# TensorE's order written by hand in three more places of a two-block layer

## The chip, the cores and the metric

The kernel runs on one core of a Trainium2 chip. Time is the device time of one execution in microseconds (us); of several runs the median counts, and the profiled execution is one further run. The engines are TensorE (PE: matmuls; PEld: its weight loads), VectorE (DVE), ScalarE (ACT), GpSimd (POOL) and the DMA queue that SyncE (SP) issues to. Each engine takes its instructions in the order in which the program has them. An instruction that waits holds up everything behind it on its engine.

## The reference, cut to what matters

512 tokens of width 1024 go through two blocks, in float32:

```python
h = h + 0.5 * swiglu(rmsnorm(h, ffn1_norm), ...)          # FFN1
h = h + (gated fox, dsa and memory attention) @ w_out     # Mix1; km, vm = split(rmsnorm(mem) @ w_mem_kv)
h = h + 0.5 * swiglu(rmsnorm(h, ffn2_norm), ...)          # FFN2

p = rms_norm(x, pre_mix_norm) @ w_in                      # Mix2: q, k, v, z of GDN; z, x, B, C, dt of SSD
q, k, v = silu(causal_dwconv(q, k, v))                    # four taps
g = -exp(gdn_a_log) * softplus(a + gdn_dt_bias)
o_a = rms_norm(gdn_chunked(l2n(q), l2n(k), v, g, beta)) * silu(z_a)
o_s = rms_norm((ssd_chunked(x, dt, B, C) + d * x) * silu(z_s))   # dt = softplus(...)
x = x + rms_norm(concat(o_a, o_s) @ w_out, post_mix_norm)
u = causal_dwconv(rms_norm(x, pre_ffn_norm) @ w_up)       # last feed-forward, ffn_conv, three taps
out = x + rms_norm((silu(gate) * up) @ w_down)
```

## The kernel before

Activations lie with the features on the 128 partitions and the 512 tokens along the free axis. Every float32 product is made of three matmuls on operands that are split into a high and a low part: `mm3` issues whi x xh, whi x xl and wlo x xh (L163, L168, L169). One such step, 128 x 128 weights on 512 tokens, is the unit in which this text counts: "a step" is three matmuls.

`wload` fetches 512 KB of weights by an SP DMA into `raw` (two buffers), ScalarE casts them to `whi` (L157) and VectorE subtracts to get `wlo` (L158). Where `k.lo` is set to `nc.gpsimd`, GpSimd makes the `wlo` instead. A block of eight steps (24 matmuls) uses one such load. SP issues its DMAs in program order too: a load that waits for a free `raw` buffer holds back every DMA behind it.

The stages, with their times in the profiled execution: FFN1 (to about 600 us), Mix1 (600 to 942), FFN2 (to 1308), Mix2 (to 1847), and `ffn_conv` (to the end). In FFN1 and FFN2, `ffn` runs 11 pairs of columns; the first pair goes through `gemm_wide`, and the norm's scale `R` is spread over the partitions by four small matmuls, `pb`. Between FFN1's pairs a generator `then` advances by one piece: setup and the loads of `mem`; `rest()`, which turns 75 rows of gains (fetched by 19 small DMAs, tile `rows`, L80 to L83) with one transpose, L88; then `mem_kv`, which transposes and splits the memory tokens (`pm`, `mm`, `my`), and makes memory keys and values.

Mix2's `gates` makes the small projections `psm`, the norm (`pn`, `ry` on GpSimd, `pb`), the softplus on VectorE (L250 to L261), `g`, its cumulative sums `pc` (four matmuls, L1400) and the table of rows `prow`. `gdn_k` and `gdn_a` make the keys and the 8 decay tables `A`, from which `blocks32` inverts small triangles on GpSimd by way of DRAM; `inverses` goes on from there on TensorE (`p1` at L1586). Then come the scans, the SSD part, the norms, the gates by `z` (whose product with `q` or `xs` is on GpSimd), the split of the result into `oa` and `os`, and `w_out`. `ffn_conv` opens with another norm.

What sets the order: everywhere but in Mix1 the framework's scheduler orders each engine's instructions by priorities that follow the order of the code; Mix1 has its TensorE order written out, under `manual_schedule`, with small pieces between product steps. Under `manual_schedule(engines={PE})` TensorE follows the code literally.

Of the kernel before, what the change touches and what calls it, by code (L numbers as in the profile page):

```python
# [4 lines left out]

# [6 lines left out]
F32R = mybir.dt.float32r  # L12
# [15 lines left out]
class K:  # L28
# [150 lines left out]
    def gemm_steps(self, w, c0, ncols, x, evac, kmax=4, after=None):  # L179

        nk = len(x)
# [81 lines left out]
    def sumsq(self, xs):  # L263

        nc = self.nc
        acc = None
        for x in xs:
            sq = self.tmp("sq")
            nc.scalar.activation(sq, x, AF.Square)
            if acc is None:  # L270
                acc = sq
            else:
                nc.vector.tensor_add(acc, acc, sq)
        return [acc]
# [53 lines left out]
    def ffn(self, h, gain, wg, wu, wd, norms=None, then=iter(())):  # L328
# [18 lines left out]
        for f0 in range(0, nff, 2):  # L347
# [16 lines left out]
            if f0 == 0:  # L364
                self.gemm_wide([(wg, 0), (wu, 0)], y, (ev_gate, ev_up), rows())
            else:
                self.gemm_fm(wg, f0 * 128, 256, y, ev_gate)
                self.gemm_fm(wu, f0 * 128, 256, y, ev_up)
            next(then, None)
# [147 lines left out]
class Mix1:  # L517
# [428 lines left out]
    def turned_evac(self, out, R):  # L946
# [4 lines left out]
        def ev(m, ps):  # L951
            t = k.tmp("vf")[:, :nb * 128]
            nc.vector.tensor_mul(t, ps[:, :nb * 128], R)
            pt = k.ps("tv")
            for b in range(nb):
                nc.tensor.transpose(pt[:, b * 128:(b + 1) * 128], t[:, b * 128:(b + 1) * 128], k.ident)
            nc.scalar.copy(out[:, :, m * 128:(m + 1) * 128], pt[:, :nb * 128].rearrange("p (b c) -> p b c", b=nb))
# [13 lines left out]
    def mem_kv(self, xt):  # L971
# [4 lines left out]
        for c in range(DC):  # L976
# [9 lines left out]
            y.append((hi, lo))  # L986
        r = k.norm_of(k.token_sumsq(xt), D)
        yield
        Rm = k.spread(r)
        kmt = k.kt.tile([128, 4, ml], F32, name="km")  # L990
# [8 lines left out]
        self.head_norm(km, self.head_stats(km, 4, 128, 128), 128, k.c("mqg"))  # L999
        self.km = km  # L1000
        vmt = k.kt.tile([128, 2, 512], F32, name="vm")
        yield from self.gemm_half(w, 512, 512, y, self.turned_evac(vmt, Rm))
# [272 lines left out]
class Mix2:  # L1275
# [25 lines left out]

    def ztile(self):
# [41 lines left out]
    def row(self, i=None, pick=None):  # L1344


        ps = self.k.ps("row", "r")
# [21 lines left out]
    def gates(self):  # L1369
# [7 lines left out]
        self.rt = k.norm_of(k.row_sums(k.sumsq(self.h)), D)  # L1377
        self.R = k.spread(self.rt)
        f = k.tmp("smf")
        nc.scalar.copy(f[:32], ps[:32])  # L1380
        pt = k.ps("smt")
# [14 lines left out]
        k.load_consts("cums")  # L1396
        pc = k.ps("pc")
# [29 lines left out]
        pt = k.ps("prow")  # L1427
# [5 lines left out]
        nc.vector.tensor_copy(self.pick, k.c("pick"))  # L1433

# [4 lines left out]
    def gdn_k(self, hf):  # L1439
        k, nc, a = self.k, self.nc, self.a  # L1440
        self.st[hf] = {"k": []}
# [7 lines left out]
        k.gemm_fm(a["w_in_2"][0], 1024 + hf * 512, 512, self.y, ev_k)  # L1449

    def gdn_qv(self, hf):
        k, nc, a = self.k, self.nc, self.a
        win = a["w_in_2"][0]
        st = self.st[hf]
        st["q"], st["v"] = qt, vb = self.big("q"), self.big("vb")

        def ev_q(m, ps):
            self.gconv(hf * 4 + m, ps, qt[:, m])

        def ev_v(m, ps):  # L1460
            t = k.tmp("vf", tag="f")
            self.gconv(16 + hf * 4 + m, ps, t)
            pt = self.turned(t, "a")
            for b in range(NB):
                nc.scalar.activation(vb[:, m, b * 128:(b + 1) * 128], pt[:, b * 128:(b + 1) * 128], AF.Copy,
                                     scale=self.vscale[:, b, hf * 4 + m:hf * 4 + m + 1])

        k.gemm_fm(win, hf * 512, 512, self.y, ev_q)
        k.gemm_fm(win, 2048 + hf * 512, 512, self.y, ev_v)

    def gdn_a(self, hf):
        k, nc = self.k, self.nc
        st = self.st[hf]
        ks = st["k"]

        (x, xv), (r, rv), (t, tv), (_, b2) = (self.per_head("kn" + c) for c in "xrtb")
        st["kd"] = []
        for m in range(4):

            pt, kd = self.turned(ks[m], "b"), k.tmp("kd", tag="kd")  # L1480
            self.sums_turned(xv[:, :, m:m + 1], pt)
            for b in range(NB):
                s = slice(b * 128, (b + 1) * 128)
                nc.scalar.activation(kd[:, s], pt[:, s], AF.Copy, scale=self.dec[:, b, hf * 4 + m:hf * 4 + m + 1])
            st["kd"].append(kd)
# [8 lines left out]
        for m in range(4):  # L1494
            hh = hf * 4 + m
# [3 lines left out]
            nc.scalar.activation(d1, d1, AF.Exp, scale=-1.0)  # L1499
            pkk = k.ps("pkk", "b")  # L1500
            for b in range(NB):
# [3 lines left out]
                                               op0=ALU.mult, op1=ALU.mult)  # L1505

    def gdn_qe(self, hf):

        k, nc = self.k, self.nc
        st = self.st[hf]  # L1510
        qt = st["q"]
        st["qe"] = qe = self.per_head("qe")[0]
        x, xv = self.per_head("qx")
        for m in range(4):
            self.sums_turned(xv[:, :, m:m + 1], self.turned(qt[:, m], "b"))
        nc.vector.tensor_scalar(qe, x, EPS, 128.0 * EPS, op0=ALU.add, op1=ALU.mult)

    def gdn_qk(self, hf):
        k, nc = self.k, self.nc
        st = self.st[hf]  # L1520
# [502 lines left out]
```

## Time and profile before

| | us |
|---|---|
| runs | 2233.55, 2235.99, 2236.47 |
| median | 2235.99 |
| profiled execution | 2238.18, of which its span 2236.5 |
| TensorE busy | 2173.7 (97% of the span) |
| VectorE busy | 1255.2 (56%) |
| ScalarE busy | 933.8 (42%) |
| GpSimd busy | 325.1 (15%) |
| mean granted clock of TensorE | 0.991 |

The busy time is the sum of an engine's instructions; what is missing to the span is time in which it waits. The granted clock is 1.00 at 2.4 GHz and 0.50 at 1.2 GHz. Views used here are the list of waits (who waited for whom, summed), the timeline (instructions in order of time, with the idle time before each and what ended it), and the windows (busy time of each engine in a given stretch).

### The profile page before, as it was taken

The page shows a single profiled execution, that of the slowest core. Times are in us where ns is not written, and L with a number is a line of the kernel's source. Part 1 is how long each engine was busy: PE and PEld are TensorE (multiplying, and loading weights), DVE is VectorE, ACT ScalarE, POOL GpSimd, SP SyncE. Part 2 cuts the span into 40 slices and gives each one's busy share as a digit, 9 for nine tenths or more (in the row PEclk, how much of TensorE's full clock was granted, in tenths as well). Part 3 has the DMA queues.
Part 4 walks back from the last instruction along what each step waited for, and adds up shares of the span by engine and source line. Part 5 has one row for each costly group of instructions (what it writes and reads, how often), then busy time and mean ns, then how long its engine had stood idle before and what let it go on. Part 6 is the DMA issues. An engine that isn't in the chain of part 4 may idle for free. (4 is left out here: it accounts for less than half of the span.)

```text
span 2236.5 us, 27895 instructions
## 1 busy us (share of the span) xinstructions
PE 2173.7 (97%) x10700; PEld 1759.4 (79%) x10700; DVE 1255.2 (56%) x2155; ACT 933.8 (42%) x1537; POOL 325.1 (15%) x340
## 2 busy tenths in 40 slices
PE   8999999999999999999999999999999898999998
PEld 6788888777677777788888877878777787888887
DVE  4544433575699654544343347866677526777623
ACT  4333322355555444332322237554556525444421
POOL 0110100011122222011110021550312100000000
PEclk9999999999999999999999999999999998999999
DMA  4233333322222223333333332331122223333332
GB/s 152 86 113 104 95 109 113 94 67 69 69 85 72 66 76 95 113 89 102 95 95 108 113 88 76 86 111 39 56 67 57 76 94 113 95 96 103 95 94 94
DMA packets 198508, 202.39 MB, mean 90 GB/s; under 512 B 19556, under 2 KB 184063, under 8 KB 198375
## 3 DMA queue, kind: packets, MB, share of 16 engines
q1 hardware_dynamic: 197607, 198.12, 29.8%
q0 software_dynamic: 768, 2.49, 0.4%
q8 instruction: 84, 1.38, 0.3%
q14 instruction: 49, 0.40, 0.1%
HBM read 192.70 MB, written 7.88 MB: 90 GB/s over the span
## 5 line engine op out<-in xcount | busy, mean ns | idle before, releaser
L163 PE MATMUL pg<-yh,whi 128*128 128x512 f32 x1856 | 745.6, 402 | 5.9 <-ACT yh L225 2.3
L169 PE MATMUL pg<-yh,wlo 128*128 128x512 f32 x1856 | 730.2, 394 | 1.2 <-DVE wlo L158 1.1
L168 PE MATMUL pg<-yl,whi 128*128 128x512 f32 x1856 | 729.7, 393 | 0.0
L158 DVE TENSOR_TENSOR wlo<-raw,whi 128x1024 fp32r<-128x1024 f32 x341 | 423.7, 1243 | 517.7 <-ACT whi L157 513.7
L157 ACT CAST whi<-raw 128x1024 fp32r<-128x1024 f32 x349 | 362.1, 1038 | 633.2 <-PE pg L168 429.7
L163 PEld LDWEIGHTS pg<-yh,whi 128*128 128x128 f32 x1856 | 350.3, 189 | 81.7 <-issue 9.1
L169 PEld LDWEIGHTS pg<-yh,wlo 128*128 128x128 f32 x1856 | 349.9, 189 | 75.4 <-DVE wlo L158 2.9
L168 PEld LDWEIGHTS pg<-yl,whi 128*128 128x128 f32 x1856 | 350.3, 189 | 67.5 <-issue 2.5
L163 PE MATMUL pg<-hidh,whi 128*128 128x512 f32 x352 | 138.7, 394 | 0.0
L169 PE MATMUL pg<-hidh,wlo 128*128 128x512 f32 x352 | 138.0, 392 | 0.0
L168 PE MATMUL pg<-hidl,whi 128*128 128x512 f32 x352 | 136.6, 388 | 0.0
L361 POOL TENSOR_TENSOR hp<-ut,sg 128x512 f32<-128x512 f32 x44 | 73.3, 1667 | 424.1 <-DVE ut L359 399.5
L217 ACT CAST hidh<-hp 128x512 fp32r<-128x512 f32 x44 | 27.3, 620 | 142.5 <-POOL hp L361 142.3
L169 PEld LDWEIGHTS pg<-hidh,wlo 128*128 128x128 f32 x352 | 66.1, 188 | 15.5
L1910 DVE SCALAR_TENSOR_TENSOR fo<-ft,fcw,fo 128x511 f32<-128x511 f32 x88 | 65.8, 749 | 21.7 <-ACT fo L1907 20.5
L168 PEld LDWEIGHTS pg<-hidl,whi 128*128 128x128 f32 x352 | 66.1, 188 | 14.8
L163 PEld LDWEIGHTS pg<-hidh,whi 128*128 128x128 f32 x352 | 66.2, 188 | 13.1
L218 DVE TENSOR_TENSOR hidl<-hp,hidh 128x512 fp32r<-128x512 f32 x44 | 30.4, 691 | 79.6 <-ACT hidh L217 79.6
L715 POOL TENSOR_SCALAR s<-s,den 128x256 f32<-128x256 f32 (+3 forms) x80 | 42.5, 533 | 190.6 <-DVE den L714 180.0
L1951 PE MATMUL pd<-whi,hidh 128*128 128x512 f32 x176 | 69.4, 394 | 0.0
L1952 PE MATMUL pd<-whi,hidl 128*128 128x512 f32 x176 | 69.4, 394 | 0.0
L1953 PE MATMUL pd<-wlo,hidh 128*128 128x512 f32 x176 | 69.2, 396 | 0.0
(502 smaller groups left out, 3000.1 us busy)
## 6 DMA issues: line engine op xcount, KB each, us to landing
raw<-in_w_in SPq DMA_DIRECT2D x100, 512.0 KB
raw<-in_ffn_w_gate SPq DMA_DIRECT2D x40, 512.0 KB
raw<-in_ffn_w_up SPq DMA_DIRECT2D x40, 512.0 KB
raw<-in_ffn_w_down SPq DMA_DIRECT2D x40, 512.0 KB
raw<-in_w_up SPq DMA_DIRECT2D x40, 512.0 KB
raw<-in_w_out SPq DMA_DIRECT2D x24, 512.0 KB
raw<-in_w_down SPq DMA_DIRECT2D x22, 512.0 KB
raw<-in_w_branch SPq DMA_DIRECT2D x12, 512.0 KB
```

The source lines that it names most:

```text
L157: nc.scalar.copy(hi, raw)
L158: (self.lo or nc.vector).tensor_sub(lo, raw, hi.bitcast(F32))
L163: first = mm(out, whi, xhi, start=start, stop=False)
L168: mm(out, whi, xlo, start=False, stop=False)
L169: mm(out, wlo, xhi, start=False, stop=stop)
L218: nc.vector.tensor_sub(lo, x, hi.bitcast(F32))
L361: nc.gpsimd.tensor_mul(p, ut, sg[m])
L715: nc.gpsimd.tensor_scalar(p[:, :w], p[:, :w], den, 1.0, op0=ALU.mult, op1=ALU.mult)
L1910: nc.vector.scalar_tensor_tensor(o[:, s:], t[:, :T - s], k.fcw[:, j:j + 1], o[:, s:], op0=ALU.mult, op1=ALU.add)
L1951: nc.tensor.matmul(pss[b], xh[:, s], hi[:, i], start=st, stop=False)
L1952: nc.tensor.matmul(pss[b], xl[:, s], hi[:, i], start=False, stop=False)
L1953: nc.tensor.matmul(pss[b], xh[:, s], lo[:, i], start=False, stop=sp)
```

## The change

FFN1's pairs from the second on are under `manual_schedule`, and `then` advances after each block of 24 matmuls instead of after each pair. The transposes of the memory values are put off by a block. Mix2's whole TensorE order is by hand: a generator `products` yields after each of 544 steps, `fill(n)` runs n of them, and small pieces stand between, directly or by `later(n, ...)`, which calls a piece n steps on. A scan makes the next state (`sc4`) before its output (`sc3`). `gdn_z(0)` and `ssd_gemms(0)` have their `wlo` on GpSimd as well: 20 such loads instead of 8. `oa` and `os` have exchanged the buffers that they are split into. At the end of Mix2, 7 matmuls of 512 columns whose result is not used (`idle`) stand ahead of `pb`, and 8 behind it. In `ffn_conv` the opening is under `manual_schedule`, its sum of squares is added up on GpSimd (7 adds), and the transposes `ph` stand between steps. TensorE's matmuls grow from 9909 to 9924, which are these 15; all others are the same ones in another order. ScalarE loads its function tables 44 times instead of 38.

```diff
 def ffn(..., then=iter(()), woven=False):
...
+        self.gemm_wide([(wg, 0), (wu, 0)], y, pair(0), rows())
+        next(then, None)
+        with self.tc.manual_schedule(engines={mybir.EngineType.PE}) if woven else ExitStack():
+            for f0 in range(2, nff, 2):
+                for w, ev in zip((wg, wu), pair(f0)):
+                    self.gemm_fm(w, f0 * 128, 256, y, ev, then=then if woven else iter(()))
...
 def turned_evac(self, out, R, turns):
...
+            def turn():
...
+            turns.append(turn)
...
 class Mix2:
+    def later(self, n, do):
+        at = self.done + n
+        i = sum(d[0] <= at for d in self.due)
+        self.due.insert(i, (at, do))
...
 def gates(self):
...
+        k.load_consts("cums")
+        yield
+        self.rt = k.norm_of(k.row_sums(acc), D)
+        yield
+        self.R = k.spread(self.rt)
...
         nc.vector.tensor_mul(g, self.dt, k.nega.unsqueeze(1).to_broadcast([128, NB, 24]))
-        k.load_consts("cums")
-        pc = k.ps("pc")
+        yield
+        pc = k.ps("pc", "b")
...
+    def idle(self, n, a, b):
+        k = self.k
+        ps = k.ps("idle", "r")
+        for _ in range(n):
+            self.nc.tensor.matmul(ps, a[0][:, :128], b[0], start=True, stop=True)
...
+        self.later(n, decay)
+        self.later(n + 2, table)
...
 def run(self):
...
+        def products():
+            k.lo = nc.gpsimd
+            yield from self.gdn_k(0)
+            yield from self.gdn_k(1)
+            k.lo = None
+            yield from self.gdn_q(0)
+            yield from self.gdn_v(0)
+            yield from self.gdn_q(1)
+            yield from self.gdn_v(1)
+            k.lo = nc.gpsimd
+            yield from self.gdn_z(0)
+            yield from self.ssd_gemms(0)
+            k.lo = None
+            yield from self.ssd_gemms(1)
+            yield from self.gdn_z(1)
+            yield from self.ssd_z()
+            yield from k.gemm_steps(a["w_out_2"][0], 0, D, self.out, ev, nk=16)
...
+            gates = self.gates()
+            next(gates)
+            for n in (3, 6, 13, 24):
+                upto(n)
+                next(gates)
+            upto(184)
+            both = [self.inverses(hf) for hf in range(2)]
+            for _ in range(7):
+                for steps in both:
+                    next(steps, None)
+                    fill(1)
+            woven(self.gdn_scan(0))
...
+            upto(298)
+            group = self.ssd()
...
+            sums = k.row_sums(sq)
+            idle(7)
+            pb = k.spread(k.norm_of(sums, D), copy=False)
+            idle(8)
...
 def ffn_conv(k, h, y, out):
+        acc = k.sumsq(h, nc.gpsimd)
+        fill(3)
+        sums = k.row_sums(acc)
+        fill(1)
+        next(turns)
+        fill(1)
+        next(turns)
+        fill(1)
+        R = k.spread(k.norm_of(sums, D))
```

TensorE in FFN1, around the transpose of the 75 gain rows. Before, it stands after 120 matmuls behind `pb`:

```order
L163 MATMUL pg_485<-yh_195,whi_518 128x512
L168 MATMUL pg_485<-yl_196,whi_518 128x512
L169 MATMUL pg_485<-yh_195,wlo_519 128x512
L88 MATMUL rows_562<-ct_base,rows_383 128x75
L979 MATMUL pm_719<-ct_base,mt_406 128x128
L979 MATMUL pm_719<-ct_base,mt_410 128x128
L163 MATMUL pg_571<-yh_167,whi_575 128x512
```

After, it stands behind 48 matmuls, the last of them those of the second pair's first load (`whi_420`); the memory's transposes follow 24 matmuls later:

```order
L164 MATMUL pg_417<-yh_179,whi_420 128x512
L169 MATMUL pg_417<-yl_180,whi_420 128x512
L170 MATMUL pg_417<-yh_179,wlo_421 128x512
L89 MATMUL rows_448<-ct_base,rows_383 128x75
L164 MATMUL pg_416<-yh_183,whi_459 128x512
L169 MATMUL pg_416<-yl_184,whi_459 128x512
L170 MATMUL pg_416<-yh_183,wlo_460 128x512
```

The transpose has moved 72 matmuls towards the start. Its DMAs stand where they stood, on SP behind the fourth load of the second pair.

VectorE in Mix2's gates, from the softplus's reciprocal (`spc`) to `g`, on which `pc` waits. Before, one `cx` (the first key's product times `R`) stands between:

```order
L253 RECIPROCAL spc_10662<-spc_10662 128x96
L254 TENSOR_TENSOR spc_10662<-spc_10662,spb_10661 128x96
L255 TENSOR_TENSOR spd_10663<-spc_10662 128x96
L256 TENSOR_SCALAR spe_10664<-spd_10663 128x96
L258 SCALAR_TENSOR_TENSOR spe_10664<-spe_10664,spd_10663 128x96 x6
L259 SCALAR_TENSOR_TENSOR spe_10664<-spe_10664,spc_10662 128x96
L261 SCALAR_TENSOR_TENSOR dt<-spe_10664,spa_10660 128x96
L1293 TENSOR_TENSOR cx_10777<-pg_10726,R_10641 128x512
L1394 TENSOR_TENSOR g_10681<-dt,nega 128x96
```

After, from the same reciprocal:

```order
L254 RECIPROCAL spc_10699<-spc_10699 128x96
L1317 TENSOR_TENSOR cx_10745<-pg_10640,R_10680 128x512
L255 TENSOR_TENSOR spc_10699<-spc_10699,spb_10698 128x96
L256 TENSOR_TENSOR spd_10700<-spc_10699 128x96
L257 TENSOR_SCALAR spe_10701<-spd_10700 128x96
L259 SCALAR_TENSOR_TENSOR spe_10701<-spe_10701,spd_10700 128x96
L1320 SCALAR_TENSOR_TENSOR kf_10744<-cx_10745,gcw,kf_10744 128x511
L259 SCALAR_TENSOR_TENSOR spe_10701<-spe_10701,spd_10700 128x96
L1320 SCALAR_TENSOR_TENSOR kf_10744<-cx_10745,gcw,kf_10744 128x510
L259 SCALAR_TENSOR_TENSOR spe_10701<-spe_10701,spd_10700 128x96
L1320 SCALAR_TENSOR_TENSOR kf_10744<-cx_10745,gcw,kf_10744 128x509
L259 SCALAR_TENSOR_TENSOR spe_10701<-spe_10701,spd_10700 128x96 x3
```

Two more rows of the softplus and then `g` follow. The `cx` has moved ahead of most of the softplus, and three of the key's convolution taps (`kf`) now stand inside it.

TensorE at `pc`. Before:

```order
L163 MATMUL pg_10804<-yh_10529,whi_10808 128x512
L168 MATMUL pg_10804<-yl_10530,whi_10808 128x512
L169 MATMUL pg_10804<-yh_10529,wlo_10809 128x512
L163 MATMUL pg_10804<-yh_10533,whi_10808 128x512
L1400 MATMUL pc_10685<-g_10681,ct_10683 128x96 x4
```

After, where `pg_10640` is the product that `cx` reads:

```order
L164 MATMUL pg_10640<-yh_10560,whi_10728 128x512
L169 MATMUL pg_10640<-yl_10561,whi_10728 128x512
L170 MATMUL pg_10640<-yh_10560,wlo_10729 128x512
L164 MATMUL pg_10641<-yh_10548,whi_10728 128x512
L169 MATMUL pg_10641<-yl_10549,whi_10728 128x512
L170 MATMUL pg_10641<-yh_10548,wlo_10729 128x512
L1435 MATMUL pc_10755<-g_10718,ct_10634 128x96 x4
```

Between `pn` and `pc` there are 30 product matmuls now and were 52, and the product that `cx` reads ends three matmuls ahead of `pc`, where it ended 16 ahead.

TensorE at the end of Mix2. Before, the last products of `w_out`, the norm's sums, the spread of its scale, and the first product of `ffn_conv`:

```order
L168 MATMUL pg_14996<-osl_14565,whi_15089 128x512
L169 MATMUL pg_14996<-slots_14543,wlo_15090 128x512
L288 MATMUL pn_15126<-ones,sq_14710 128x1 x4
L321 MATMUL pb_15142<-ct_base,ry_15139 128x128 x4
L163 MATMUL pg_15222<-yh_15153,whi_15229 128x512
```

After:

```order
L170 MATMUL pg_15001<-osh_14645,wlo_15095 128x512
L289 MATMUL pn_15131<-ones,sq_14715 128x1 x4
L1476 MATMUL idle_15143<-osh_14553,slots_14305 128x512 x7
L322 MATMUL pb_15155<-ct_base,ry_15152 128x128 x4
L1476 MATMUL idle_15160<-osh_14553,slots_14305 128x512 x8
L164 MATMUL pg_15247<-yh_15176,whi_15254 128x512
```

(`pn` has a second row of four in both.) The two groups `idle` stand where TensorE had nothing.

## Rows read from the trace of the kernel before

**Rows 1.** Windows, four stretches: elapsed, busy time by engine (x instructions), granted clock, DMA.
```profile
600.00:942.50 342.50, 337.89 (x1770) 265.65 (x1771) 234.02 (x580) 172.25 (x336) 79.82 (x113) 1.00 0.28 83
942.50:1307.80 365.30, 363.71 (x1604) 299.19 (x1603) 139.79 (x164) 104.54 (x129) 39.16 (x23) 1.00 0.33 98
1307.80:1847.00 539.20, 518.25 (x2974) 417.08 (x2973) 357.03 (x618) 286.09 (x529) 139.45 (x137) 0.99 0.26 75
1331.00:1405.80 74.80, 70.40 (x355) 56.92 (x356) 58.92 (x143) 54.83 (x145) 11.68 (x5) 1.00 0.25 71
```
**Rows 2.** List of waits, PE, 34.3 to 205.9 (total us, times, longest).
```profile
PE pg L169 <- DVE wlo L158: 1.1, 3, 0.5
PE hs L605 <- ACT hq L602: 1.1, 1, 1.1
PE pm L979 <- DVE mm L981: 1.0, 2, 0.5
```
**Rows 3.** List of waits, PE, 1307.8 to 1847.
```profile
PE pg L168 <- DVE oal L218: 4.7, 1, 4.7
PE tr L1341 <- POOL q L1670: 3.2, 5, 1.5
PE tr L1341 <- ACT vf L1298: 2.6, 2, 2.4
...
PE tr L1341 <- ACT kf L1298: 1.9, 1, 1.9
PE pc L1400 <- DMA ct<-in_consts: 1.6, 1, 1.6
```
**Rows 4.** List of waits, PE, 1847 to 1898.6.
```profile
PE pb L321 <- POOL ry L244: 3.5, 2, 1.7
```
**Rows 5.** Windows at half clock (columns as in rows 1).
```profile
171.40:174.80 3.40, 3.40 (x18) 3.40 (x17) 2.87 (x11) 0.46 (x1) 0.00 (x0) 0.50 0.04 7
...
1765.40:1772.20 6.80, 4.07 (x10) 3.20 (x11) 3.90 (x6) 1.36 (x2) 0.00 (x0) 0.50 0.00 0
1850.80:1861.00 10.20, 6.35 (x16) 4.84 (x17) 7.80 (x15) 4.74 (x8) 1.01 (x1) 0.50 0.79 272
```
**Rows 6.** Timeline, PE: start, duration, instruction, idle before it and what ended it.
```profile
2.86 0.24 PE L88 MATMUL rows<-ct_base,rows 8*128 8x8 f32 x1 [2.86 <-DMA rows<-in_ffn_norm]
...
31.84 0.60 PE L321 MATMUL pb<-ct_base,ry 128*128 128x128 f32 x4
...
206.10 0.44 PE L956 MATMUL tv<-ct_base,vf 128*128 128x128 f32 x2 [1.44 <-DVE vf L953]
```
**Rows 7.** Timeline, SP's queue (issues) in FFN1 and behind the last table.
```profile
1.25 0.35 SPq L83 DMA_DIRECT2D rows<-in_ffn_norm  x1
...
47.59 0.25 SPq L81 DMA_DIRECT2D rows<-in_dsa_k_norm  x1
...
1405.86 0.35 SPq L1552 DMA_DIRECT2D ascr<-A  x1
```
**Rows 8.** Timeline, DVE in Mix2's gates.
```profile
1322.66 0.26 DVE L254 TENSOR_TENSOR spc<-spc,spb 128x96 f32<-128x96 f32 x1
...
1323.49 3.80 DVE L258 SCALAR_TENSOR_TENSOR spe<-spe,spd 128x96 f32<-128x96 f32 x6
...
1333.67 0.73 DVE L1296 SCALAR_TENSOR_TENSOR kf<-cx,gcw,kf 128x511 f32<-128x511 f32 x1
```
**Rows 9.** Groups of instructions, DVE, 1307.8 to 1847: total busy, mean ns of one.
```profile
L158 DVE TENSOR_TENSOR wlo<-raw,whi 128x1024 fp32r<-128x1024 f32 x61 | 77.9, 1277 | 74.1 <-ACT whi L157 73.2 <-PE pg L169 0.5
...
L1504 DVE SCALAR_TENSOR_TENSOR A<-pkk,knb,d 128x128 f32<-128x128 f32 x32 | 9.7, 345 | 1.4 <-PE pkk L1503 0.9
L1359 DVE TENSOR_TENSOR d<-row,pk 128x256 f32<-128x256 f32 x24 | 9.4, 417 | 0.8 <-PE row L1350 0.8
```
**Rows 10.** Timeline, POOL in Mix2: one weight split, and the last loads of `blocks32`.
```profile
1324.18 2.40 POOL L158 TENSOR_TENSOR wlo<-raw,whi 128x1024 fp32r<-128x1024 f32 x1 [4.95 <-ACT whi L157]
...
1483.90 1.56 POOL L1572 DMA_DIRECT2D X<-xscr  x2
```

More of the change, by code (lines that the diff above doesn't have):

```diff
@@ L326, in spread, with ffn @@
         return r
-    def ffn(self, h, gain, wg, wu, wd, norms=None, then=iter(())):
+    def ffn(self, h, gain, wg, wu, wd, norms=None, then=iter(()), woven=False):
         nc = self.nc
@@ L346, in ffn, with pair @@
         hid = [None] * nff
-        for f0 in range(0, nff, 2):
+        def pair(f0):
             sg = {}
@@ L953, in ev @@
             nc.vector.tensor_mul(t, ps[:, :nb * 128], R)
[L954 to L957, printed above, removed]
+            def turn():
+                pt = k.ps("tv")
+                for b in range(nb):
+                    nc.tensor.transpose(pt[:, b * 128:(b + 1) * 128], t[:, b * 128:(b + 1) * 128], k.ident)
+                nc.scalar.copy(out[:, :, m * 128:(m + 1) * 128], pt[:, :nb * 128].rearrange("p (b c) -> p b c", b=nb))
+            turns.append(turn)
         return ev
@@ L1707, in ssd, with group @@
         free = self.slots()
-        for g in range(2):
+        def group(g):
             bm, cm = self.bc[g], self.bc[2 + g]
@@ L1764, in ssd_z @@
+        return group
     def ssd_z(self):
@@ new lines, in run, with fill, upto, woven @@
+        work = products()
+        def fill(n):
+            for _ in range(n):
+                next(work, None)
+                self.done += 1
+                while self.due and self.due[0][0] <= self.done:
+                    self.due.pop(0)[1]()
+        def upto(n):
+            fill(n - self.done)
+        def woven(steps):
+            for n in steps:
+                fill(n)
+        with self.tc.manual_schedule(engines={mybir.EngineType.PE}):
+            gates = self.gates()
[10 more added lines that the diff above has]
+            woven(self.gdn_scan(0))
+            for m in range(4):
+                self.gdn_qk(1, m, 5 * m)
+            fill(19)
+            woven(self.gdn_scan(1))
+            for hf in range(2):
+                self.gdn_norm(hf)
+                for m in range(4):
+                    self.later(16 + 10 * hf + 2 * m, partial(self.gdn_out, hf, m))
+            upto(298)
+            group = self.ssd()
+            for g in range(2):
+                woven(group(g))
+            free, tags = self.slots(F32R), iter(("A", "QK", "A", "kd") * 4)
+            def slot(s):
+                tag = next(tags)
+                return next(free) if tag == "A" else k.tmp(s, F32R, tag)
+            self.out += [k.split(self.st[hf]["q"][:, m], "oa", slot) for hf in range(2) for m in range(4)]
+            upto(416)
+            self.out += [k.split(x, "os", k.yslot) for x in self.xs[:4]]
+            upto(544)
+            idle = lambda n: self.idle(n, self.out[0], self.out[8])
+            sums = k.row_sums(sq)
+            idle(7)
+            pb = k.spread(k.norm_of(sums, D), copy=False)
+            idle(8)
@@ L1911, in conv, with pair @@
         return o
-    for f0 in range(0, nff, 2):
+    def pair(f0):
         sg = {}
@@ L1927, in ev_up, with products, fill @@
             hid[f0 + m] = k.split(o, "hid", (lambda s: k.hslot(s, F32R)) if f0 + m < 4 else None)
-        if f0 == 0:
-            k.gemm_wide([(w, 0), (w, DFF)], y, (ev_gate, ev_up), rows())
-            residual()
-        else:
-            k.gemm_fm(w, f0 * 128, 256, y, ev_gate)
-            k.gemm_fm(w, DFF + f0 * 128, 256, y, ev_up)
+        return ev_gate, ev_up
+    def products(f0):
+        for c0, ev in zip((0, DFF), pair(f0)):
+            yield from k.gemm_steps(w, c0 + f0 * 128, 256, y, ev)
+    with k.tc.manual_schedule(engines={mybir.EngineType.PE}):
+        work, turns, pss = products(2), residual(), []
+        k.gemm_wide([(w, 0), (w, DFF)], y, (lambda m, ps: pss.append(ps),) * 2)
+        def fill(n):
+            for _ in range(n):
+                next(work, None)
+        acc = k.sumsq(h, nc.gpsimd)
[7 more added lines that the diff above has]
+        R = k.spread(k.norm_of(sums, D))
+        for ev, two in zip(pair(0), (pss[:2], pss[2:])):
+            for m, ps in enumerate(two):
+                ev(m, ps)
+                fill(1)
+                next(turns, None)
+        fill(1000)
+        for _ in turns:
+            pass
+    for f0 in range(4, nff, 2):
+        for _ in products(f0):
+            pass
     wd = a["w_down_2"][0]
```

332 lines of the change are left out of this document (175 added, 157 removed).

## The prediction, made before the changed kernel was run

> **What bounds the kernel now.** I read the page's busy shares first: TensorE works 97% of the span, so what can be won is its waiting, its half-clock stretches and the switching between products and small work; all product steps stay. The windows by stage come next [rows 1]. FFN2, which the change leaves alone, shows the price of pure products: 365.3 us for 1604 matmuls, or 0.228 us each, 1.6 us idle. Mix1, whose order is by hand, idles 4.6 us of 342.5 (1.35%); Mix2 idles 539.2 - 518.25 = 20.95 us (3.9%). Then the lists of waits, which say who ends that idle time [rows 2 to 4]: an operand that VectorE, ScalarE or GpSimd hands over late, each time with ready products standing behind it in the order. Last the windows at half clock [rows 5]: after such waits TensorE is granted 0.50, that is 1.2 GHz, for 3.4 us or a multiple. The row from 171.4 stands for four of 3.4 us (the others begin at 1478.7, 1594.8 and 1884.9). TensorE busy for t us at half clock loses t/2: 1.7 us for each of the four, 2.0 for the one from 1765.4 (4.07 busy), 3.2 for the one from 1850.8 (6.35 busy).
>
> **FFN1.** What goes: the waits for wlo 1.1, hq 1.1 and mm 1.0 [rows 2], tv's 1.44 [rows 6], and the half clock from 171.4, 1.7: together 6.3. I take all of it, since 24 products (5.5 us) now lie between a memory piece and its reader. What comes: a wait at the transpose of the gain rows. TensorE leaves `pb` at about 32 [rows 6] and has 48 matmuls of 0.228, 10.9 us, before it: it arrives at 43. The last of the 19 small loads is issued at 47.59 and takes 0.25 [rows 7]; SP's order up to there is the old one, and these loads stand behind the second pair's fourth weight load, whose buffer depends on VectorE and not on TensorE's later order. From issue to use, a load of the same kind took 2.86 - 1.25 = 1.6 us [rows 6, 7]. So the rows arrive near 49.3 and TensorE waits about 6 us (4.8 if they landed at once). Before, this cost nothing, because 72 more matmuls (16.4 us) stood ahead. Clock behind it: the 4.7 us wait for `oal` [rows 3] was followed by the 2.0 us of half-clock loss [rows 5]; I take 2. Sum: 6 + 2 - 6.3 = +2 (from -5, if the loads are early after all, to +5, if the memory's denser weight loads make TensorE wait too).
>
> **Mix2, what goes.** The five large waits, oal 4.7, q 3.2, vf 2.6, kf 1.9, ct 1.6 [rows 3], are 14.0 of the 20.95. Of the other 7 I let 4 go; one that stays is the first, for FFN2's last output. The oal wait goes because the late half of the result is now last in `w_out`'s contraction; the ct wait because its load is issued earlier; the others because steps stand in between. Half clock: 1.7 + 1.7 + 2.0 = 5.4. Together -23.4.
>
> **Mix2, what comes.** First `pc`: the key's product ends three matmuls (0.7 us) ahead of it, and then VectorE has one `cx` and three taps at about 0.73, and twelve small operations from the reciprocal to `g` at about 0.28 (one is 0.26, with a little between them) [rows 8]: 2.9 + 3.4 = 6.3 us. TensorE waits some 6 us with all products behind it on the same in-order engine (3.4 us if the taps come out behind `g`, 8 if a GpSimd split falls into it, below); clock, 2. Second, `blocks32`: its chain runs from the first issue behind the last table at 1405.86 [rows 7] to the end of the last issue at 1485.5 [rows 10] and the landing, some 82 us, and TensorE's order puts 95 steps (65 us) and about 12 us of small matmuls between the last table and `p1`: a wait of 3 (0 to 6), plus 1.7 for the clock. Third, VectorE, where it has as much to do as TensorE: the tables of the k part and the SSD's first group. I set 5 (0 to 14), from the next paragraph. Sum +17.7. Net Mix2: -6 (-20 to +8). The inverses, which now alternate between the halves with a step between, and the scans I cost at nothing: products cover them, and without that cover each of their 14 pieces would show a copy of well under 1 us.
>
> **GpSimd beside VectorE.** Six softplus operations took 3.80 us where one takes 0.26 [rows 8]: while GpSimd made a weight split from 1324.18 to 1326.58 [rows 10], one of them was held for 2.2 us. Twelve more splits go to GpSimd: each takes 1.28 us off VectorE [rows 9] and may hold an operation for up to 2.2, so 12 x 0.9 = 11 us more VectorE time at worst, 15 less at best. That is where the 0 to 14 above comes from, with a further 3 us for the SSD group's denser tables; 5 is the middle of what a path that is VectorE's in parts would show.
> The Trainium skill (GPSIMD Engine Reference, Specifications) says that GpSimd shares its SBUF interfaces with VectorE and contends with VectorE instructions that have two SBUF inputs, and that speaks against this part of the change. By that rule, the trace agrees: the held operation reads two tensors. Were every split to hold VectorE on TensorE's path, the sum would be 6 us worse; were none to, 5 better.
>
> **End of Mix2 and the opening.** What goes: the second of the two waits for `pb` (half of 3.5 [rows 4]), now behind 9 products and two transposes; the half clock from 1884.9, 1.7, and from 1850.8, 3.2, if the 15 idle matmuls keep the clock up. They shorten no chain: 7 x 0.228 = 1.6 us fits into the first `pb` wait of 1.7. If the clock has already fallen when they run, they take twice that, and the two groups delay the path by 1.3 and about 1.2. What comes: the seven adds on GpSimd, which contend with VectorE while it makes `ffn_conv`'s operands: 1.5 (0 to 5). Net -5 (-6.6 to +1.5).
>
> **Sum.** +2 - 6 - 5 = -9 against the profiled execution's 2238.2, or 2229. That execution lies 2.2 us above the median of the runs, 2236.0; I forecast a median of 2227.
>
> **Rivals.**
> (a) The hand order works as in Mix1. For: it is the same method, and Mix1 idles 1.35%. Mix2 would then idle 7.3 instead of 20.95, -13.7, with its half clock gone, -5.4; FFN1 -6.3; the opening -6.6. Sum -32: 2204. Against: Mix1 had no step like `pc`, three matmuls behind its operand. Chance 0.18.
> (b) Slower: the decay tables are VectorE's. Eight tables come at every third step, that is 9 matmuls, 2.05 us, and two small ones, 2.6 in all. For one table VectorE makes two `d` (0.83), a clamp and four `A` (1.4) [rows 9], about 2.6, and beside it convolution and weight work. Before, TensorE pulled products forward; in a fixed order it cannot, and the PSUM bank of `pkk` is the stop. If VectorE is 1.5 us behind at each of the eight tables, that is 12, with clock losses of 2 and a contended `pc` (+2): 2227 + 16 = 2243. It decides as soon as VectorE needs over 1 us per table beside the table. Against: in the k part before, VectorE was busy 58.9 of 74.8 us [rows 1], which leaves room. Chance 0.18.
> (c) The idle matmuls do nothing or harm: the clock falls anyway. The opening gives -1 instead of -5, a little less than the second `pb` wait. 2231. Chance 0.15.
> (d) New waits pay back all that the old ones cost, 2236 (the two new waits of 6 us at their upper ends and `blocks32` at 6). Chance 0.13.
>
> **How the numbers follow.** My forecast, 2227, gets 0.36. The range reaches to (a) and over (b): 2206 to 2246. A measurement of this kernel tells about 0.2%, 4.5 us, from no change. Faster by more than that, below 2231.5: the forecast nearly whole (0.34), (a) 0.18, half of (c) 0.08, and a little of (d), 0.61. Within it: the rest of (c), most of (d), a part of (b), 0.20. Slower: 0.19.
>
> **What would show it.** In the profile after: a TensorE wait of about 6 us at `rows` (L89) near 43 us, ended by a DMA, and one of about 6 at `pc` (L1435), ended by VectorE's `g`, each with a half clock behind; no wait for `oal`, `vf` or POOL `q` over 1 us; a full clock through the end of Mix2, with the yh wait filled. I am wrong if `rows` doesn't wait (the loads were then issued earlier than the order suggests), if the table stretch in the k part shows TensorE waiting for `A` eight times (b), or if Mix2 is shorter by 15 us or more (a).

## The result, and the profile after

The changed kernel takes 2297.8 us (median of four runs, 2296.5 to 2300.7); the kernel before takes 2235.7 in the same series. The ratio is 1.028, with a 95% interval of 1.0265 to 1.029: slower by 62 us, where the prediction had 9 us faster.

The stages, read off the timelines, each from its first matmul to that of the next (us; FFN1 counts from the start of the span, and the last column runs from the final `pn` of the second mixer to the last matmul):

| | FFN1 | Mix1 and FFN2 | Mix2 | opening and end |
|---|---|---|---|---|
| before | 415.8 | 893.3 | 541.3 | 379.0 |
| after | 419.2 | 894.8 | 599.0 | 375.3 |

The first matmul of Mix1 is at 415.8 us in the kernel before; the 600 us that were given for it above are wrong, so the window from 600 to 942.5 in [rows 1] is only the later part of Mix1. The whole of it, from 415.8, idles 13.8 us of 526.7 (2.6%).

Nearly everything came in the second mixer. The windows of the kernel after (elapsed, busy time by engine, granted clock, DMA share, GB/s): the first feed-forward's first part, the second mixer, and in it the stretch of the decay tables.

```profile
34.30:205.90 171.60, 163.45 (x814) 137.91 (x813) 78.70 (x116) 56.94 (x83) 18.97 (x13) 0.96 0.35 105
1312.80:1909.80 597.00, 535.92 (x2974) 434.11 (x2973) 354.17 (x606) 294.95 (x535) 165.84 (x149) 0.95 0.24 68
1362.50:1448.90 86.40, 64.27 (x238) 49.72 (x237) 45.88 (x113) 46.46 (x112) 4.78 (x2) 0.80 0.13 38
```

The second line answers to the third of [rows 1]. The same 2974 matmuls took 597.0 us instead of 539.2, 57.8 more. TensorE was idle for 597.0 - 535.9 = 61.1 us, before 20.95: 40.1 more. And the matmuls themselves took 535.9 - 518.25 = 17.7 more, since the granted clock is 0.95 on the mean; in the stretch of the tables it is 0.80. VectorE's busy time has hardly changed (354 against 357), though 12 weight splits, some 15 us, have left it: other operations of its own took longer. One that takes 0.74 us elsewhere took 2.18 while GpSimd made a split:

```profile
1380.24 2.37 POOL L159 TENSOR_TENSOR wlo<-raw,whi 128x1024 fp32r<-128x1024 f32 x1 [11.07 <-ACT whi L158]
1380.98 2.18 DVE L1320 SCALAR_TENSOR_TENSOR kf<-cx,gcw,kf 128x511 f32<-128x511 f32 x1
```

What TensorE waited for in the second mixer (us in total, times, longest), to be held against [rows 3]; `tr` are the transposes of keys, values and `x` (`kf`, `vf`, `xs`) behind their convolutions:

```profile
PE pkk L1538 <- DVE A L1539: 22.5, 24, 3.5
PE tr L1371 <- ACT vf L1322: 6.8, 3, 4.2
PE pc L1435 <- DVE g L1429: 6.4, 1, 6.4
PE tr L1371 <- ACT xs L1324: 6.3, 3, 4.3
PE tr L1371 <- ACT kf L1322: 4.7, 3, 2.5
PE pn L289 <- DVE sq L274: 3.7, 2, 2.3
PE row L1381 <- DVE xdt L1778: 2.9, 2, 2.7
```

The waits for `oal`, for GpSimd's `q` and for the constants `ct` are gone, as was forecast. In their place stands one that the list of before has with 1.3 us: 24 waits at `pkk`, three for each of the eight decay tables. For a table TensorE multiplies a head's keys with themselves in four quarters of one PSUM tile, `pkk`, and VectorE scales each quarter into `A`. One table, on TensorE and then on VectorE (start, duration, instruction, idle before it and what ended it):

```profile
1397.03 0.38 PE L1538 MATMUL pkk<-kf 128*128 128x128 f32 x2
1399.66 0.49 PE L1538 MATMUL pkk<-kf 128*128 128x128 f32 x2 [2.25 <-DVE A L1539]
1400.59 0.80 PE L1538 MATMUL pkk<-kf 128*128 128x128 f32 x2 [0.45 <-DVE A L1539]
1401.83 0.80 PE L1538 MATMUL pkk<-kf 128*128 128x128 f32 x2 [0.44 <-DVE A L1539]
```

```profile
1398.12 1.23 DVE L159 TENSOR_TENSOR wlo<-raw,whi 128x1024 fp32r<-128x1024 f32 x1 [1.05 <-ACT whi L158]
1399.26 0.35 DVE L1539 SCALAR_TENSOR_TENSOR A<-pkk,knb,d 128x128 f32<-128x128 f32 x1
1400.19 0.35 DVE L1539 SCALAR_TENSOR_TENSOR A<-pkk,knb,d 128x128 f32<-128x128 f32 x1 [0.58 <-PE pkk L1538]
1401.43 0.35 DVE L1539 SCALAR_TENSOR_TENSOR A<-pkk,knb,d 128x128 f32<-128x128 f32 x1 [0.89 <-PE pkk L1538]
```

The two engines hand the four quarters of one table to and fro. The code writes matmul, operation, matmul, operation, all on one PSUM tile, and each matmul from the second on carries a wait for the operation before it. A turn takes 0.93 us (1399.66 to 1400.59; the same in another table, from 1392.09, at a granted clock of 1.00) and 1.24 at half clock (1400.59 to 1401.83). But the turns are the smaller part of the 22.5 us. The first wait of each table, 0.5 to 3.5 us and 14.9 for the eight, is for a VectorE that is late: here a weight split, for which VectorE itself waited 1.05 us, stands ahead of its first operation. The other sixteen waits make 7.6 us. In both cases TensorE stands, because the hand order has nothing between the four matmuls. The scheduler of the kernel before had put products there (`pg` in this stretch of its trace, which has several tables in it):

```profile
1368.07 0.86 PE L1503 MATMUL pkk<-kf 128*128 128x128 f32 x6
1368.68 0.48 PE L169 MATMUL pg<-yh,wlo 128*128 128x512 f32 x1
1369.00 0.64 PE L1503 MATMUL pkk<-kf 128*128 128x128 f32 x4
1369.39 0.48 PE L163 MATMUL pg<-yh,whi 128*128 128x512 f32 x1
1369.71 0.38 PE L1503 MATMUL pkk<-kf 128*128 128x128 f32 x2
```

### The profile page after: what moved, and what is told of

Read it like the earlier page. It is cut to its first block, busy times and chain, and to the rows that moved or that the text cites. A ratio compares the mean times of both kernels' runs of the same rounds, so it can differ in the third digit from the quotient of the medians.

```text
span 2295.6 us, 27889 instructions
## 1 busy us (share of the span) xinstructions
PE 2195.2 (96%) x10715; PEld 1779.4 (78%) x10715; DVE 1253.8 (55%) x2136; ACT 942.2 (41%) x1543; POOL 363.7 (16%) x359
## 4 chain that ended last, share of the span: by engine, by line
PE 83%; DVE 9%; ACT 4%; issue 2%; POOL 1%; DMA 1%; SPq 0%; DVEq 0%; POOLq 0%; ACTq 0%
PE pg L164 23%; PE pg L169 22%; PE pg L170 22%; PE pd L2129 2%; PE pd L2128 2%; PE pd L2127 2%; DVE wlo L159 1%; ACT whi L158 1%; PE po L728 1%; PE pt L710 1%; DVE kf L1320 1%; DVE xs L1320 1%; DVE cx L1317 1%; PE pkk L1538 1%; PE tr L1371 1%
## 5 line engine op out<-in xcount | busy, mean ns | idle before, releaser
L164 PE MATMUL pg<-yh,whi 128*128 128x512 f32 x1856 | 762.7, 411 | 3.2 <-ACT qk L751 2.0
L159 DVE TENSOR_TENSOR wlo<-raw,whi 128x1024 fp32r<-128x1024 f32 x329 | 408.4, 1242 | 496.7 <-ACT whi L158 493.4
L164 PEld LDWEIGHTS pg<-yh,whi 128*128 128x128 f32 x1856 | 355.1, 191 | 79.4 <-issue 10.3
L169 PEld LDWEIGHTS pg<-yl,whi 128*128 128x128 f32 x1856 | 355.1, 191 | 71.9 <-issue 3.4
L2057 DVE SCALAR_TENSOR_TENSOR fo<-ft,fcw,fo 128x511 f32<-128x511 f32 (+1 forms) x88 | 65.6, 749 | 17.9 <-ACT fo L2054 16.7
```

Of the source, the lines that this page charges most:

```text
L159: (self.lo or nc.vector).tensor_sub(lo, raw, hi.bitcast(F32))
L164: first = mm(out, whi, xhi, start=start, stop=False)
L169: mm(out, whi, xlo, start=False, stop=False)
L2057: nc.vector.scalar_tensor_tensor(o[:, s:], t[:, :T - s], k.fcw[:, j:j + 1], o[:, s:], op0=ALU.mult, op1=ALU.add)
```

## The experiments

T1 is the theory of these round trips: TensorE stands because matmul and operation alternate. Its rivals are that VectorE is late because GpSimd's weight splits hold it (T2), and that any fixed order waits at whatever is late (T3). The differences shown are against the changed kernel unless another is named. Each run's text of expectation is what was on record ahead of it.

**The round trips taken out (e1_pkk).**

```diff
             for b in range(NB):
                 s = slice(b * 128, (b + 1) * 128)
                 nc.tensor.matmul(pkk[:, s], ...)
+            for b in range(NB):
+                s = slice(b * 128, (b + 1) * 128)
                 nc.vector.scalar_tensor_tensor(st["A"][:, m * NB + b], pkk[:, s], ...)
```

> The changed kernel, but each decay table's four pkk matmuls stand ahead of its four VectorE operations A instead of alternating with them. Theory T1 (round trips: since the four share one PSUM tile, each matmul of a table waits for the A before it, and by hand no product stands between them): the 24 waits of 22.5 us go, and most of the half clock that follows them between 1362 and 1448 us (24 us at 0.5, so up to 12): 2298 falls to about 2268. Theory T2 (VectorE is late in itself, held by GpSimd's weight splits): the waits move to the next reader, the time falls by 5 us at most. Theory T3 (any fixed order waits at whatever is late): a third of it comes back as other waits, 2280.

Measured 2263.4 us, 34 less. The list has 1.7 us at `pkk` instead of 22.5:

```profile
PE tr L1371 <- ACT vf L1322: 6.8, 4, 4.3
PE tr L1371 <- ACT kf L1322: 6.8, 3, 3.5
PE pc L1435 <- DVE g L1429: 6.4, 1, 6.4
PE tr L1371 <- ACT xs L1324: 6.1, 3, 4.3
...
PE pkk L1538 <- DVE A L1541: 1.7, 2, 0.8
```

```profile
1311.00:1878.00 567.00, 522.11 (x2972) 426.34 (x2973) 350.88 (x606) 293.45 (x534) 163.24 (x149) 0.97 0.23 71
```

The mixer's window is 30 us shorter, of which 16.2 are idle time (44.9 left) and 13.8 faster matmuls: with the waits most of the half clock went. Of the 20.8 us that went at `pkk`, some 4.6 came back elsewhere (2.5 at `pkq`, the next reader of `A`, and 2.1 more for `kf`), not the third that T3 has; and the time fell by far more than the 5 us of T2. What the edit removed is TensorE's standing, not VectorE's lateness. The first table, on TensorE and on VectorE:

```profile
1368.91 1.05 PE L1538 MATMUL pkk<-kf 128*128 128x128 f32 x8
1373.20 1.11 DVE L1541 SCALAR_TENSOR_TENSOR A<-pkk,knb,d 128x128 f32<-128x128 f32 x4
```

VectorE begins 4.3 us behind TensorE, in the changed kernel it was 3.5, but TensorE goes on with products and the next tables meanwhile. So the alternation is the cause of these 34 us; VectorE's lateness is what it made TensorE pay for.

**The gain rows two blocks later (e2_rows).** Two more `yield` ahead of `rest()`.

> The changed kernel, but the transpose of the gain rows, and the memory's work behind it, come two blocks (48 matmuls, 10.9 us) later in the first feed-forward. T1 and the prediction's step on this wait: the 5.9 us wait at rows goes and so does the half clock behind it (6.8 us at 0.5, 3.4 lost): 2298 falls by about 8, to 2290. If the time hangs on the memory's chain and not on this wait: no change.

Measured 2296.0, 2 less. The wait at the rows is gone. In the first feed-forward there came others:

```profile
PE hs L612 <- ACT hq L609: 3.7, 2, 2.2
PE pb L322 <- POOL ry L245: 2.0, 1, 2.0
PE pg L170 <- DVE wlo L159: 1.3, 2, 0.8
PE pg L164 <- ACT whi L158: 0.7, 1, 0.7
```

The stage became 2.1 us shorter only. So the step "one wait, one gain" is not settled by this run: two blocks move the memory's norm (`pb`) and its heads' sums (`hs`) against their own operands. The profile shows a further thing. The second mixer, which this edit leaves alone, took 606 us in it against 599 in the changed kernel's, with nearly the same waits, 7 us of it in the matmuls' own time. So a few us in one stage can't be read from the total of this kernel.

**`pc` seven steps later (e3_pc).** `for n in (3, 6, 20, 31)` instead of `(3, 6, 13, 24)`.

> The changed kernel, but pc comes at step 20 instead of 13 and prow at 31 instead of 24. If the 6.4 us wait at pc stands for itself, 7 steps of 0.686 us cover 4.8 of it and half of the 3.4 us lost at half clock: 2298 falls by about 6, to 2292. If VectorE bounds this part (T2), the wait moves to the key's transpose and the tables: 2297 or more.

Measured 2300.2, 2 more, with the runs of the two kernels overlapping. The wait at `pc` shrank from 6.4 to 4.2, and two key transposes now wait 6.2 us together, 4.7 of it at one of them; all waits for `kf` had been 4.7. Moving that one reader alone gains nothing. The likely reason, not tested, is that the next piece reads what the same chain on VectorE and ScalarE makes afterwards.

**The 12 further splits back on VectorE (e4_splits).** `k.lo = nc.gpsimd` ahead of `gdn_z(0)` left out.

> The changed kernel, but the 12 weight splits of gdn_z(0) and ssd_gemms(0) are VectorE's again (8 on GpSimd instead of 20). T2: VectorE is no longer held, the waits for vf, xs, sq and xdt between 1460 and 1830 us (some 20 us) shrink by half or more: 2298 falls by 10 or more. T1: these have another cause, VectorE has 12 x 1.24 = 15 us more to do there: between -3 and +5.

Measured 2297.5, no difference. As the kernel stands, GpSimd's splits cost nothing and bring nothing. VectorE's busy time in the mixer rose by 6 us only (360.3 against 354.4), not by the 15 that 12 splits take: with fewer splits on GpSimd its other operations were faster.

**Longer lags (e5_lags, on e1_pkk).**

```diff
-            for n in (3, 6, 13, 24):
+            for n in (3, 6, 20, 31):
...
-            self.later(10, lambda: self.gdn_kt(hf, m))
+            self.later(14, lambda: self.gdn_kt(hf, m))
...
-            self.later(9, lambda: turn(m, t))
+            self.later(11, lambda: turn(m, t))
```

(And 14 for 11 at the query norms, 12 and 15 for 8 and 11 at the SSD norms.)

> e1_pkk, and the small pieces of the second mixer stand further behind the products that they read: key transposes 14 steps instead of 10, query norms 14 for 11, value and x transposes 11 for 9, SSD norms 12 and 15 for 8 and 11, pc at step 20 and prow at 31 for 13 and 24. Theory L (the pieces stand too close: the chain product, cx, four taps, table load, Silu on two engines takes longer than 9 or 10 steps, 6 to 7 us, while VectorE as a whole is only 69% busy): the waits of 26 us for vf, kf, xs, q and sq shrink by about half, and some half clock goes: 2263 falls to about 2248. Theory V (VectorE itself is the bound in these stretches): the waits move behind the next product, no change beyond 4 us.

Measured 2270.0: three runs between 2269.6 and 2273.0, and one of 2252.1. Against the text, three of the four are slower than e1_pkk. But the profile (of the run of 2273.0) shows that the waits of the theory did go, and what came for them:

```profile
PE p L1659 <- DMA A<-xtscr: 14.4, 2, 12.8
PE tr L1371 <- ACT vb L1581: 3.6, 2, 2.5
PE pkk L1538 <- DVE A L1541: 2.8, 3, 1.8
PE tr L1371 <- ACT kf L1322: 0.8, 1, 0.8
PE tr L1371 <- ACT vf L1322: 0.5, 1, 0.5
```

```profile
1489.00:1550.40 61.40, 49.15 (x499) 38.64 (x500) 14.15 (x18) 10.83 (x21) 17.56 (x20) 0.50 0.16 50
1342.20:1489.00 146.80, 136.74 (x684) 112.33 (x682) 115.16 (x210) 104.22 (x271) 63.52 (x72) 1.00 0.27 79
```

From behind `pc` to `p1` the mixer ran at full clock, and came to the inverses 175.9 us after the mixer's first matmul, where e1_pkk came to them after 197.9. There it stood in front of GpSimd's chain (`blocks32`, by way of DRAM) for 12.8 us. Then, from 1499.6 to 1550.4 (the first 10.6 us of the upper window are still the wait), it ran the inverses, many small matmuls, and some products at 1.2 GHz: 51 us on end, busy for 49 of them. The inverses took 45.8 us instead of 24.8. The run of 2252.1 has no profile, but its mean granted clock is on record: 0.988, where the other three have 0.976 to 0.978. At half clock a stretch counts for half in that mean, so 0.011 is some 50 us of half clock less, by estimate: as much as the long stretch. So the lags gain 11 us against e1_pkk where the clock comes back, and lose 7 where it stays down.

**The end of the change without its idle matmuls (e6_noidle, on e1_pkk).**

```diff
             sums = k.row_sums(sq)
-            idle(7)
             pb = k.spread(k.norm_of(sums, D), copy=False)
-            idle(8)
```

> e1_pkk without the 15 idle matmuls around the spread of the norm at the end of the second mixer. If they keep the clock up, as the prediction said, the half clock comes back from the first product of the last feed-forward on, for up to 10 us of which 3.2 us are lost: 2263 rises by 2 to 4. If the clock does not hang on them: within 1 us.

Measured 2264.8 against 2263.4: the intervals of the two overlap, and the stretch from the last `pn` is 376.1 us in both. The window from 1882.4 to 1892.7, first without the idle matmuls, then with them:

```profile
1882.40:1892.70 10.30, 7.65 (x19) 5.54 (x20) 9.06 (x13) 5.22 (x9) 2.63 (x2) 0.50 0.31 108
```

```profile
1882.40:1892.70 10.30, 9.82 (x37) 7.45 (x36) 7.90 (x13) 4.94 (x8) 2.39 (x2) 0.83 0.59 200
```

They do keep the clock up in the main (0.83 against 0.50). With it TensorE reaches VectorE's `yl` early and waits 2.1 us for it, where without them it waits 0.3. What the clock gives, the operands take back.

**The end of the change alone (e7_open), the table's order alone (e8_bpkk), both (e10_combo), on the kernel before.** e7_open has the idle matmuls and `ffn_conv`'s new opening; e8_bpkk has e1_pkk's edit.

> The kernel before with the end of the change alone: the 15 idle matmuls around the norm's spread, and the last feed-forward's opening in hand order with its sum of squares on GpSimd. The profile of the changed kernel has this stretch 2.8 us shorter than before: 2236 falls to 2233. If the gain there belongs to what comes ahead (the exchanged places, the products' order), no change.

> The kernel before, but with each decay table's four pkk matmuls written ahead of the four operations A, as in e1_pkk. T1 says that the scheduler of the kernel before had put products between those matmuls and so hid the round trips: there is only the 1.3 us wait at pkk to win, 2236 falls by 0 to 3. If the alternation itself costs time wherever it stands, 10 us or more are won.

> The kernel before with the two pieces that each made it faster alone: the end of the change (idle matmuls and the opening in hand order, 2233.6 against 2236.2) and the four pkk matmuls ahead of their four operations (2232.7). They lie 400 us apart: if they add, 2236.2 - 2.6 - 3.4 = 2230.

Measured 2233.6, 2232.7 and 2231.1 against 2236.2, 2236.2 and 2235.6 for the kernel before beside them (ratios 0.9987, interval 0.9978 to 0.9997; 0.9986, 0.9976 to 0.9996; 0.9977, 0.9967 to 0.9986). Each part gains a little on its own. e8_bpkk also confirms T1 from the other side: where the scheduler puts products between, the alternation costs 3 us, where nothing stands between, 34.

**`p1` twenty steps later (e9_late, on e5_lags).** `upto(204)` for `upto(184)`.

> e5_lags with the first matmul of the inverses (p1) at step 204 instead of 184. In e5_lags the waits at the k part's pieces shrank, but TensorE then waited 14.4 us at p1 for GpSimd's chain by way of DRAM, and ran the inverses, which are small matmuls, at half clock for 61 us. Theory C (that chain of some 80 us is the next bound, and the long half clock hangs on its wait): 20 steps of 0.686 us cover 13.7 us of it, the half clock goes, 2270 falls to about 2243 (14 of waiting, 13 of the 30 us or less that the clock took). Theory V (VectorE bounds the part): the gain is the wait's 14 us at most, and other waits take half of it back: 2263.

Measured 2258.2, 12 less than e5_lags, and 6 more than its one run of 2252.1. The inverses are back at 24.8 us and the long half clock is gone. The expectation had 27, so a part came back: TensorE now waits 7.3 us for a `wlo` that GpSimd makes, ahead of `p1`, and 5.4 for `xd`, a GpSimd product.

**`pc` four more steps, the gain rows one block later (e11_best, on e9_late).** `(3, 6, 24, 35)`; one more `yield` ahead of `rest()`.

> e9_late with pc at step 24 and prow at 35 (20 and 31), and the gain rows' transpose one block later in the first feed-forward. pc's last 4.2 us of waiting and its half clock (3.4 lost) are covered by four more steps (2.7) in part: -4; the rows' wait of 5.6 us is covered by 5.5, -4 (e2_rows showed that a part comes back as waits of the memory's chain). Together 8 us below e9_late. If VectorE is what these wait for, no more than 3.

Measured 2243.1, 15 less. Most of it is the first feed-forward: 406.0 us in the profile, against 419.5 in e9_late and 415.8 in the kernel before, with no wait over 0.5 us behind its opening and a granted clock of 1.00.

**The first feed-forward's change alone (e12_ffn1), and with the rows one block later (e15_ffn1b), on the kernel before.** e15_ffn1b differs from e12_ffn1 by one line:

```diff
             xt = m.load_mem()
             yield
+            yield
             rest()
```

> The kernel before with the change of the first feed-forward alone (its pairs in hand order, the memory's work once per block). The stage was 3.4 us longer in the changed kernel's profile: 2236 rises to 2239.5. The prediction's step on it had +2.

> e12_ffn1 with the gain rows' transpose one block (5.5 us) later, nothing else. The prediction's step says that of the hand order in the first feed-forward 6.3 us are won and 8 lost at this one transpose: 2239.6 falls by 6 of waiting and 3.4 of half clock and more where the hs wait's clock goes: to 2228. e2_rows, two blocks later, had other waits (pb 2.0, hs 3.7) for it: by that pattern 2236.

Measured 2239.6 (ratio 1.0018, 1.0009 to 1.0027) and 2228.2 (0.9962, 0.9949 to 0.9974), beside 2235.6 and 2236.5 for the kernel before. One `yield` is worth 11 us: the hand order of this stage gains 8 us, and the place of one small transpose turned that into a loss of 4. The waits of the stage, first e12_ffn1, then e15_ffn1b:

```profile
PE rows L88 <- DMA rows<-in_dsa_k_norm: 5.5, 1, 5.5
PE hs L611 <- ACT hq L608: 1.8, 1, 1.8
```

```profile
PE pg L169 <- DVE wlo L158: 0.5, 1, 0.5
PE pm L990 <- DVE mm L992: 0.4, 1, 0.4
```

**The further splits on VectorE, once more (e13_dve, on e11_best).** e4_splits's edit.

> e11_best with the 12 further weight splits on VectorE again, as in e4_splits. In e11_best TensorE waits 6.5 us for a wlo of GpSimd's, which stands on GpSimd's queue behind blocks32, and 5.3 for xd, another GpSimd product of the same stretch. Theory Q (GpSimd's queue is what the splits cost here: now that p1 stands later, they lie behind the chain): both waits go, with half clock behind each, 2243 falls to about 2232. Theory P (GpSimd holds VectorE's operations by its second input): the waits of VectorE's group (L, xs, vb, some 15 us) shrink as well, 2225. If neither: VectorE has 15 us more to do, 2245.

Measured 2231.9 (0.9983, 0.9973 to 0.9992): 11 less, where the same edit did nothing in e4_splits. GpSimd's queue in e11_best and the TensorE instruction that waited for it:

```profile
1482.48 1.56 POOL L1645 DMA_DIRECT2D X<-xscr  x2
1484.05 4.67 POOL L159 TENSOR_TENSOR wlo<-raw,whi 128x1024 fp32r<-128x1024 f32 x2
```

```profile
1486.45 0.80 PE L170 MATMUL pg<-yh,wlo 128*128 128x512 f32 x1 [6.45 <-POOL wlo L159]
```

The split begins in the moment in which `blocks32` has issued its last load: it had stood behind it on GpSimd's queue. With `p1` at step 184 the products of `gdn_z(0)` came behind that chain, with 204 ahead of it. That is theory Q for the `wlo`; its other half failed, since the wait for `xd`, which was to go as well, rose from 5.3 to 7.0. Theory P is not borne out: the waits for `L`, `xs` and `vb` are the same in e13_dve (4.8, 3.1, 6.0) as in e11_best (4.8, 3.1, 5.6).

**All that helped, on the kernel before (e14_sum).** e15_ffn1b, e8_bpkk and e7_open together; the second mixer keeps the scheduler's order.

> The kernel before with the three parts of the change that help or can be mended: the first feed-forward in hand order with the gain rows one block later (e15_ffn1b), the four pkk matmuls ahead of their operations, and the opening (e10_combo, 2231). The second mixer keeps the scheduler's order. In e11_best's profile the first feed-forward was 9.8 us shorter than before: 2231 falls to about 2221. If that gain hung on the clock's phase in that run alone: 2231.

Measured 2221.5 (0.9937, 0.9925 to 0.995): faster than both kernels, 15 us below the one and 76 below the other.

## Why the prediction was wrong, step by step

**The two new waits of the order were right, to half a microsecond.** `rows`: forecast about 6, ended by a DMA, near 43 us; the profile has 5.9 from 42.8 on. `pc`: forecast about 6, ended by `g`; 6.4. The sum of the first feed-forward, +2, was measured as +3.4 in the profile and +4 alone (e12_ffn1). That the loss there is this one transpose, and that the rest gains 6 and more, is shown by e15_ffn1b.

**The step that failed is "Mix2, what comes", its third item**: "VectorE, where it has as much to do as TensorE: the tables of the k part ...: I set 5 (0 to 14)." The second mixer, put at -6 us in sum, came to +58. The tables cost 22.5 us of waiting and about 14 of half clock. Rival (b) named the place, with 12 us and a chance of 0.18, and half of the mechanism: VectorE is behind at each table, by 1.9 us on the mean in the first waits (14.9 in all), where (b) had 1.5. The stop it had wrong. Not the PSUM bank holds TensorE but each quarter's operation, a wait that the code of before contains as well; it makes TensorE pay for VectorE's lateness and adds the turns, 7.6 us. In e1_pkk, where only the bank is left as a stop, `pkk` waits 1.7 us. The text says that TensorE "pulled products forward" before, and did not ask between which instructions. A list of waits shows only what the scheduler could not hide; the 24 dependences were in the code and had no row.

**"What goes" was half right.** Of the 14.0 us of large waits [rows 3], oal, `q` from GpSimd and ct went (9.5 us). vf and kf went from 2.6 and 1.9 to 6.8 and 4.7, xs from 0.2 to 6.3, and the sums at `pn` for sq, which had not waited, to 3.7. "The others because steps stand in between" is the failed sentence: 9 or 10 steps are 6 to 7 us, and the chain of product, `cx`, taps, table load and Silu was longer. e5_lags showed it for vf and kf: with 11 and 14 steps they wait 0.5 and 0.8.

**The clock.** I let 5.4 us of half-clock loss go and put 2 + 1.7 in. It was the other way: 17.7 us more of matmul time in the mixer. The waits of 0.4 to 3.5 us close together cost more in clock than their sum: in the stretch of the tables, with 22.1 us idle, the mean granted clock of 0.80 means some 35 of 86 us at half, while the single 6.4 us wait at `pc` came with 6.8 us at half. A single wait can cost more as well, as the 12.8 us in e5_lags did.

**GpSimd.** The forecast gave the 12 splits 0 to 14 us by way of VectorE. They cost nothing where they stood (e4_splits). They cost 11 us when the schedule around them moved (e13_dve), and through GpSimd's own queue. The contention with VectorE that was weighed there is real: 12 splits fewer made VectorE's busy time shorter by 6 us in the changed kernel and by 3 in e11_best, not by 15. But it did not reach TensorE: the waits for VectorE are nearly the same with and without the splits.

**`blocks32`** was put at 3 us (0 to 6). The chain was sized rightly (83.5 us from the first issue to the end of the last in the changed kernel). But TensorE took 89 us from the last table to `p1`, where 77 were forecast; 9 of them are waits for vf and q. So the chain showed nothing, in e1_pkk neither. In e5_lags these waits were gone, and it was 12.8 us and the half clock after it.

**The opening** was put at -5 and is -3.7 in the profile, -2.6 alone (e7_open). The idle matmuls keep the clock up as forecast and are worth nothing that could be measured (e6_noidle); both `pb` waits went.

**Rival (a)** was priced too low. Its 1.35% is the idle share of the later part of Mix1; the whole stage has 2.6%, which would leave Mix2 with 14 us of idle time and the rival at 2211 instead of 2204.

**What stays open.** e13_dve's second mixer, in hand order with five mends, still takes 550.5 us against 541.3. Its largest waits are for `xd` (7.0), `vb` (6.0) and `L` (4.8). Why they are late was not tried. Nor was the exchange of `oa` and `os` tested by itself.

## What to carry to other kernels

Before an order is fixed by hand, look in the code for pieces that alternate between two engines on one tile: a scheduler hides their round trips and the lateness of the second engine, a hand order shows every one, and the list of waits of the old kernel has almost no row for them. Write the producer's instructions in a row and the consumer's behind them, set each lag by the measured chain and not by the engine's busy share, and look where the last of a group of small DMAs lands before a transpose is moved forward. And mend one thing at a time but judge them together: longer lags alone made this kernel slower in three runs of four, because the next chain came into view, and the same edit on GpSimd's splits was worth nothing in one schedule and 11 us in another.

## What the runs showed of the hardware that was not expected

A round trip of a 128 x 128 matmul and a 128 x 128 VectorE operation on its result took 0.93 us, of which 0.35 is the operation. Behind a wait of 12.8 us TensorE stayed at 1.2 GHz for 51 us, busy for 49 of them with some 500 matmuls, most of them small: half clock is not always a matter of 3 or 7 us. And a stretch that idle matmuls held at a mean clock of 0.83 ended no sooner than the same stretch at 0.50, since its operands came at VectorE's pace. While GpSimd made a weight split, a VectorE operation on two tensors took 2.18 us that elsewhere takes 0.74.
